# Mixer of a hybrid decoder step: PSUM banks divided 2/2/2/2 instead of 3/2/2/1

## The chip, the core and the metric

The kernel runs on one core of one Trainium2 chip. The metric is the device time of one execution in microseconds. The time before is 2019.17 us, the median of three runs (2019.03 to 2019.56).

## The reference

One decoder layer is applied to a prompt of 1024 positions and to 8 samples of 4 new positions each, 1056 rows of 1024 values:

```python
x = _layer_norm(ALPHA * x + 0.5 * _swiglu(x, ffn1_w_in, ffn1_w_out), ln1_g, ln1_b)
h = x @ w_in
q, k, v, u_b, v_b = jnp.split(h, [D_A, 2 * D_A, 3 * D_A, 3 * D_A + D_B], axis=-1)
# A: 8 heads x 64, windows (128, 512, 2048) at dilations (1, 4, 16), combined by their denominators
# B: u * (W_s LN(v) + b) over chunks of 128 positions, W_s lower-triangular
mixed = jnp.concatenate([_rms_norm(o_a, out_a_g), _rms_norm(o_b, out_b_g)], axis=-1) @ w_out
x = _layer_norm(ALPHA * x + mixed, ln2_g, ln2_b)
x = _layer_norm(ALPHA * x + 0.5 * _swiglu(x, ffn2_w_in, ffn2_w_out), ln3_g, ln3_b)
```

For the samples, the keys and values of 1024 past positions come from a cache. The outputs are the final rows, the key and value rows of the prompt, the shifted caches of the samples and the normalised `v_b` rows of the samples. All of it is float32.

## The kernel before

Three stages follow each other: the first feed-forward block (`ffn(1, ...)`), the mixer (`mixer`), and the output projection with the second feed-forward block. Each dense product is split into a rounded high part and a remainder, so that one product becomes three matmuls on TensorE (`mm3`, line 272).

PSUM has eight banks of 128 x 512 float32. `bank(use)` hands one out. Outside the mixer all eight carry the tag `acc` and are given in turn. In the mixer, `open_banks(self.split)` divides them by use. A bank is free again when its last reader has finished; the next tile of the same tag waits for that.

- `acc` (3 banks): everything that isn't attention proper. The projections of queries and keys (`qk_pair`), of values and of both halves of the gate (`tok_proj`, 24 matmuls into one bank, issued in four parts with other work between them), the gate's spatial product (`mix`, line 943), the transposes of `finish` and `key_rows`, all the work on the samples (`samples`: transposes of cached keys, two score banks s0 and s1 that are held together, transposed probabilities, an output bank), half of the output projection (`out_b`), and the sums for the normaliser (`chunk`, line 1561).
- `sc` (2): scores of the attention (line 1109), read by VectorE with the mask's logarithm added and the row maximum taken (line 1110).
- `pt` (2): probabilities transposed on TensorE (line 1157), then split into high part and remainder by ScalarE and VectorE (lines 1162 to 1169).
- `po` (1): output products of the attention (`pv`, line 1135). One tile collects all key blocks of one head and one 256-wide block of positions; the upper 64 partitions are copied out by ScalarE (line 1143) and added to the lower 64 by VectorE (line 1144). There are 8 heads and 4 blocks, so 32 such tiles.

In `uproj(0)`, for each block of 128 positions, the product's bank stays open while `mix` fills a second one. VectorE adds the bias to mix's result (line 945), and then multiplies the product into it (line 954).

What runs beside what is set by generators. `mixer` walks through `attention`, and for each of its steps advances two others: `dense()` (the projections in the order of `ORDER`) and `windows()` (the samples of the four pairs of heads, once the gate is finished). Each yields an estimated cost, and `ratio`, `ratio2` and `ratio3` set how much of the two is issued for each unit of attention. That gives the order in which the instructions are written. The order in which each engine then gets them is made when the program is built, by the framework's scheduler: it takes the written order as a priority, and an instruction whose tile has no free bank is put back behind others that can go. So the number of banks also has a part in the order of the instructions. The order by hand (`manual_schedule`) is used only for the last rows of the second feed-forward block.

At the end of the mixer, `mix_norm` normalises the attention's result in three chunks of columns, while the last products of `out_b` run.

Of the kernel before, what the change touches and what calls it, by code (L numbers as in the profile page):

```python
# [99 lines left out]
class Net:  # L100
# [1296 lines left out]
            nc.scalar.activation(self.xh[:, 4 + q, :], o[:], AF.Copy)  # L1397
            nc.vector.tensor_sub(self.xl[:, 4 + q, :], o[:], self.xh[:, 4 + q, :].bitcast(F32))  # L1398

    split = {"acc": 3, "sc": 2, "pt": 2, "po": 1}  # L1400
    ratio, ratio2, ratio3 = 5.0, 0.7, 0.7

    def run(self):
# [200 lines left out]
```

## Time and profile before

| what | value |
| --- | --- |
| median of three runs | 2019.17 us |
| the profiled execution | 2019.33 us |
| its span | 2017.5 us |
| instructions | 39560 |
| matmuls | 15775 |
| DMA traffic | 339.65 MB |
| POOL (GpSimd) busy | 140.0 us (7%) |

The profile gives, for one execution, the busy time of each engine: PE is TensorE's matmuls, PEld its weight loads, DVE VectorE, ACT ScalarE, POOL GpSimd and SP SyncE, which issues most DMAs. A group of instructions is named by its line in the kernel, its engine and "out<-in", with the names of the tiles that it writes and reads. Start times are in microseconds from the start of the span. In a row of a timeline, the number in brackets is how long the engine had been idle before the instruction, with the instruction that released it. Matmuls are pipelined, so the duration of a single one is longer than the distance between two.

The mixer lies at about 745 to 1228 us of the span.

### The profile page before, as it was taken

Reading aid. Unit: us, or ns where it says so; the run is one execution under the profiler, and the core shown is the slowest. Engines: PE = TensorE matmul, PEld = TensorE weight load, DVE = VectorE, ACT = ScalarE, POOL = GpSimd, SP = SyncE. Lnnn points to the kernel's source line nnn. Section 1 sums busy time; section 2 is a strip of 40 time slices with the busy share of each in tenths; the row PEclk is TensorE's granted clock in tenths of the full one; section 3 lists DMA queues with packets and bytes.
Section 4 is the critical chain, followed back from the end, with each engine's and each line's share of the span. In section 5 each row is a group of like instructions: output and inputs, shape, how many; then the busy total and the mean of one; then the engine's idle time right before and its main releaser. Section 6 shows DMA issues by size and latency. Waiting matters only on the chain.

```text
span 2017.5 us, 39560 instructions
## 1 busy us (share of the span) xinstructions
PE 1978.6 (98%) x15775; PEld 1919.1 (95%) x15775; DVE 1405.6 (70%) x3196; ACT 825.0 (41%) x1696; POOL 140.0 (7%) x221
## 2 busy tenths in 40 slices
PE   8999999999999999999999899999999999999998
PEld 7999999999999989999898788999999999999997
DVE  5777767777767853846546768767677776777678
ACT  4334333432222373325646653763434343313223
POOL 0000000000000001313213320000000000000003
PEclk9999999999999999999999999999999999999999
DMA  8246454559455243112544755223545655684732
GB/s 236 75 164 214 168 196 170 202 201 346 190 214 193 85 138 102 43 45 87 173 149 141 232 181 177 86 68 103 199 173 192 221 175 196 240 342 143 264 103 108
DMA packets 246823, 339.65 MB, mean 168 GB/s; under 512 B 11699, under 2 KB 205151, under 8 KB 240991
## 3 DMA queue, kind: packets, MB, share of 16 engines
q1 hardware_dynamic: 245399, 333.36, 47.9%
q10 hardware_dynamic: 1240, 3.76, 0.5%
q8 instruction: 124, 2.03, 0.4%
q14 instruction: 60, 0.49, 0.1%
HBM read 238.18 MB, written 132.45 MB: 184 GB/s over the span
## 4 chain that ended last, share of the span: by engine, by line
PE 89%; DVE 6%; DMA 2%; ACT 2%; issue 1%; SPq 0%; POOL 0%; ACTq 0%; DVEq 0%; POOLq 0%
PE acc L511 40%; PE acc L272 21%; PE acc L611 16%; PE acc L479 4%; PE po L1135 2%; PE sc L1109 2%; PE pt L1157 1%; DVE st L376 1%; PE acc L1222 1%; DVE row L791 1%; PE acc L1264 1%; PE acc L305 1%; PE acc L367 0%; DMA tmp<-obT 0%; PE acc L1228 0%
## 5 line engine op out<-in xcount | busy, mean ns | idle before, releaser
L198 ACT ACTIVATE wh<-raw 128x512 fp32r<-128x512 f32 (+1 forms) x528 | 285.3, 551 | 560.0 <-PE acc L611 155.2
L511 PE MATMUL acc<-xo,wh 128*128 128x264 f32 x2560 | 466.7, 283 | 2.3 <-ACT wh L198 1.8
L199 DVE TENSOR_TENSOR wl<-raw,wh 128x512 fp32r<-128x512 f32 (+1 forms) x528 | 311.0, 595 | 130.3 <-ACT wh L198 125.7
L511 PEld LDWEIGHTS acc<-xo,wh 128*128 128x128 f32 x2560 | 394.3, 188 | 3.0 <-ACT wh L198 2.2
L511 PE MATMUL acc<-xo,wl 128*128 128x264 f32 x1280 | 361.2, 283 | 0.0
L511 PE MATMUL acc<-xq,wh 128*128 128x264 f32 x1920 | 350.8, 283 | 0.0
L611 PE MATMUL acc<-gc,wh 128*128 128x264 f32 x1792 | 329.8, 285 | 0.0
L511 PEld LDWEIGHTS acc<-xq,wh 128*128 128x128 f32 x1920 | 295.9, 188 | 0.0
L611 PEld LDWEIGHTS acc<-gc,wh 128*128 128x128 f32 x1792 | 279.3, 189 | 0.2
L511 PE MATMUL acc<-xq,wl 128*128 128x264 f32 x960 | 271.2, 283 | 0.0
L611 PE MATMUL acc<-gc,wl 128*128 128x264 f32 x896 | 255.8, 285 | 0.0
L511 PEld LDWEIGHTS acc<-xo,wl 128*128 128x128 f32 x1280 | 242.0, 189 | 0.0
L511 PEld LDWEIGHTS acc<-xq,wl 128*128 128x128 f32 x960 | 181.6, 189 | 0.0
L611 PEld LDWEIGHTS acc<-gc,wl 128*128 128x128 f32 x896 | 168.5, 188 | 0.0
L272 PE MATMUL acc<-xh,wh 128*128 128x384 f32 (+2 forms) x416 | 134.3, 325 | 4.4 <-ACT xh L1397 2.1
L272 PE MATMUL acc<-xl,wh 128*128 128x384 f32 (+2 forms) x416 | 130.4, 313 | 0.2 <-DVE xl L1398 0.2
L272 PE MATMUL acc<-xh,wl 128*128 128x384 f32 (+2 forms) x416 | 130.0, 313 | 0.0
L272 PE MATMUL acc<-wh,xh 128*128 128x256 f32 (+1 forms) x432 | 122.2, 283 | 0.2 <-ACT tmp L1078 0.2
L272 PE MATMUL acc<-wl,xh 128*128 128x256 f32 (+1 forms) x432 | 121.7, 282 | 0.0
L272 PE MATMUL acc<-wh,xl 128*128 128x256 f32 (+1 forms) x432 | 121.0, 280 | 0.0
L479 PE MATMUL acc<-xq,wh 128*128 128x264 f32 x512 | 99.2, 293 | 3.1 <-ACT wh L198 2.2
L622 DVE TENSOR_TENSOR z<-acc,z 128x264 f32<-128x264 f32 x200 | 83.6, 430 | 21.4 <-PE acc L611 21.0
(223 smaller groups left out, 3558.4 us busy)
## 6 DMA issues: line engine op xcount, KB each, us to landing
gc<-gst SPq DMA_DIRECT2D x112, 528.0 KB
raw<-ffn_w_in SPq DMA_DIRECT2D x88, 512.0 KB
gc<-gc SPq DMA_DIRECT2D x40, 1056.0 KB
raw<-ffn_w_out SPq DMA_DIRECT2D x44, 512.0 KB
gc<-gc SPq DMA_DIRECT2D x32, 528.0 KB
out_ksmp<-cache_k SPq DMA_DIRECT2D x8, 2040.0 KB
out_vsmp<-cache_v SPq DMA_DIRECT2D x8, 2040.0 KB
raw<-w_in SPq DMA_DIRECT2D x20, 512.0 KB
```

What stands on the lines that cost most here:

```text
L198: nc.scalar.activation(h, src, AF.Copy)
L199: nc.vector.tensor_sub(l, src, h.bitcast(F32))
L272: self.nc.tensor.matmul(out, s, m, start=first and i == 0, stop=last and i == n - 1)
L305: nc.tensor.transpose(p[:, r * RB:(r + 1) * RB], t[:RB, k * 128:(k + 1) * 128], self.ident[:RB, :RB])
L376: nc.vector.bn_stats(st[:n, i], ps[i][:n])
L479: nc.tensor.matmul(p, w[:, ks], x[:, z, k % 4], start=k == 0 and q == 0, stop=k == KT - 1 and q == 2)
L511: nc.tensor.matmul(p, w[:, ks], x[:, z, kk], start=new and kk == 0 and r == 0, stop=kk == 3 and r == 2, skip_group_check=True)
L611: nc.tensor.matmul(p, w[:, ks], g[:, o:o + HB], start=new and k == 0, stop=k == nk - 1, skip_group_check=True)
L622: nc.vector.tensor_add(y, p, y)
L791: nc.vector.scalar_tensor_tensor(t[:n, hs], ps[h][:n], mv[:n, 0:1], gb[:n, hs], op0=OP.subtract, op1=OP.mult)
L1109: nc.tensor.matmul(b[:, :w], st[:, i * 128:(i + 1) * 128], kk[:, c0:c0 + w], start=z == 0, stop=z == 1)
L1135: nc.tensor.matmul(out[:, :256], V[p][s][:, 2 * m + kt], x[:, kt], start=m == 0 and kt == 0 and z == 0, stop=m == j and kt == 1 and z == 1)
```

## The change

One line: the mixer's division of the eight banks. The dense products and the samples get two instead of three, the attention's output products two instead of one.

```diff
-    split = {"acc": 3, "sc": 2, "pt": 2, "po": 1}
+    split = {"acc": 2, "sc": 2, "pt": 2, "po": 2}
```

No instruction is added or removed by it, and no tile in SBUF changes. What changes is which bank a tile gets, what it waits for, and through that the order on the engines.

## The prediction

> **What bounds the kernel now.** I read the page's busy times and its chain first, then the mixer alone, since only its PSUM is touched.
>
> ```profile
> PE 1978.6 (98%) x15775; PEld 1919.1 (95%) x15775; DVE 1405.6 (70%) x3196; ACT 825.0 (41%) x1696; POOL 140.0 (7%) x221
> ...
> PE 89%; DVE 6%; DMA 2%; ACT 2%; issue 1%; SPq 0%; POOL 0%; ACTq 0%; DVEq 0%; POOLq 0%
> ```
>
> TensorE is busy 98% of the span, and 89% of the chain that ended last is its work. So time in which TensorE has nothing to issue is paid nearly in full, and a change that removes no work can win only TensorE's idle time. The next view cuts the mixer into stretches (length, then busy time of PE, PEld, DVE, ACT, POOL, the granted clock, DMA share and GB/s):
>
> ```profile
> 745.00:875.00 130.00, 128.20 (x998) 126.39 (x998) 75.55 (x225) 47.23 (x104) 31.79 (x39) 1.00 0.26 79
> ...
> 1110.00:1140.00 30.00, 24.00 (x151) 19.69 (x149) 22.85 (x57) 18.82 (x40) 10.19 (x16) 0.89 0.80 251
> ...
> sum 483.00, PE 469.72 PEld 430.28 DVE 288.05 ACT 236.73 POOL 120.31; mean PE 67.10 PEld 61.47 DVE 41.15 ACT 33.82 POOL 17.19
> ```
>
> In the mixer's 483 us TensorE is idle for 13.3 (483.00 less 469.72); 6.0 of those lie in one hole at 1110 to 1140. What it waits for there (total, times, longest):
>
> ```profile
> PE po L1135 <- DVE oa L1144: 3.1, 4, 1.0
> PE pt L1157 <- DVE pl L1163: 2.6, 3, 1.7
> PE acc L272 <- ACT xh L1397: 2.1, 2, 1.8
> PE acc L1083 <- ACT vo L996: 1.0, 1, 1.0
> ...
> PEld po L1135 <- DVE oa L1144: 4.9, 7, 1.3
> ```
>
> The first row is what the change aims at: an output product waits until L1144 has read the only po bank. It is 3.1 us in four waits; the weight loads' 4.9 us are mostly the same pauses seen one instruction earlier. The fourth row is the longest wait for an acc bank, 1.0 us once: with three of them these waits are covered.
>
> **Part 1, the second po bank.**
>
> ```profile
> L1143 ACT ACTIVATE oadd<-po x32: 380/381/383, 827.8 to 1211.8; 64x256 f32<-64x256 f32 x32
> L1144 DVE TENSOR_TENSOR oa<-po,oadd x32: 396/417/420, 830.8 to 1214.8; 64x256 f32<-64x256 f32 x32
> ```
>
> The po bank is emptied 32 times by a pair of reads of 0.38 and 0.42 us, first to last. That would be 25.6 us if TensorE stood still for each; it stood still 3.1 us, because other instructions lie between. So the gain is bounded by 0 and 4.9 us, and I take the direct row: **-3.1**. No instruction, DMA or SBUF tile is added.
>
> **Part 2, two acc banks: where the third was in use.** Every dense product, transpose and sample score of the mixer draws from acc. I go through the users in the order of the code.
>
> *Plain token products* (values, v half of the gate): bank one is read while bank two is written.
>
> ```profile
> 761.50 22.97 PE acc L272 x192
> ...
> L996 ACT ACTIVATE vo<-acc x16: 359/385/385, 760.6 to 1045.6; 128x256 f32<-128x256 f32 x16
> ```
>
> 192 matmuls in 22.97 us are 0.12 us each, 2.9 us for a product of 24. The read takes 0.385 us. Two banks cover that: **0**.
>
> *The u products of the first half* (`uproj(0)`). After each product comes `mix(n)`, which takes a second bank, and the product's own bank is read only after mix's is (L945, then L954). One of nine such places, TensorE and then VectorE:
>
> ```profile
> 879.78 1.05 PE L943 MATMUL acc<-vb,wt 128*128 128x128 f32 x8
> 880.59 0.36 PE L1135 MATMUL po<-pl,vhl 128*128 128x256 f32 x1
> ...
> 881.02 0.28 PE L272 MATMUL acc<-wh,xh 128*128 128x256 f32 x1
> ```
>
> ```profile
> 880.87 0.69 DVE L945 TENSOR_TENSOR vb<-acc,vec 128x512 f32<-128x512 f32 x1 [2.63 <-PE acc L943]
> 881.59 0.42 DVE L954 TENSOR_TENSOR vb<-acc,vb 128x256 f32<-128x256 f32 x1
> ```
>
> The next product starts at 881.02 in the third bank. With two, the first to come free is mix's, at 881.56 (880.87 and 0.69). Counted from 880.59, when mix has been issued, that is a gap of 0.97 us, nine times: 8.7. Attention work can stand in it: 0.43 us does already here. The stretch of all nine holds this much of it (scores, transposes, outputs; PE busy):
>
> ```profile
> 874.48:913.47 38.99, 2.91 (x13) 1.00 0.19 53
> ```
>
> ```profile
> 874.48:913.47 38.99, 0.98 (x6) 1.00 0.19 53
> ```
>
> ```profile
> 874.48:913.47 38.99, 1.68 (x8) 1.00 0.19 53
> ```
>
> Together 5.57 us. If all of it moved into the gaps, 3.2 us would be left over; if none could, 8.7. I take **+4**, near the lower end, since the instructions are put in order when the program is built, with the bank counts known, and most of the 5.57 us can move a few matmuls.
>
> *The samples.* `samples` takes s0 and s1 together, and VectorE reads them (L1236) when its queue comes to it. One of the eight pairs:
>
> ```profile
> 1066.96 1.28 PE L1228 MATMUL acc<-kv,qbd 128*32 128x512 f32 x16
> ...
> 1069.85 0.29 PE L272 MATMUL acc<-xh,wh 128*128 128x288 f32 x1
> ```
>
> ```profile
> 1072.01 0.67 DVE L1236 CUSTOM_DVE_ANT_0 pt<-acc,pt 128x512 f32<-128x512 f32 x1
> ```
>
> At 1069.85 a dense product runs in the third bank while both others hold scores until 1072.68. With two banks it can't start, and behind an open dense product s1 can't be written until that product has been finished and copied out. I cut out the eight stretches from the last L1228 matmul of a pair to the end of the first L1236 read, for all instructions and then for L272 alone:
>
> ```profile
> sum 39.92, PE 36.38 PEld 32.42 DVE 31.14 ACT 17.50 POOL 12.05; mean PE 4.55 PEld 4.05 DVE 3.89 ACT 2.19 POOL 1.51
> ```
>
> ```profile
> 1011.76:1024.54 12.78, 6.11 (x42) 5.45 (x42) 1.00 0.49 146
> ...
> sum 39.92, PE 15.24 PEld 13.84; mean PE 1.91 PEld 1.73
> ```
>
> In 39.9 us TensorE does 15.2 us of dense work that the change forbids or moves. Upper end: all is lost, 15.2. Lower end: 0, where the open product is drawn ahead of the pair (TensorE stays busy then) and attention fills the rest. Attention can't fill it all: VectorE, on which its next steps wait, is busy 31.14 of 39.92 us. I take half, **+8**.
>
> *The tail.* The normaliser's sum holds a bank while VectorE works through a reciprocal, and an output product waits for its read behind it:
>
> ```profile
> 1212.26 2.54 DVE L1565 RECIPROCAL ry<-ry 128x384 f32<-128x384 f32 x1
> ...
> 1215.76 0.45 DVE L860 SCALAR_TENSOR_TENSOR tmp<-tmp,acc 128x288 f32<-128x288 f32 x1
> ```
>
> ```profile
> 1212.62 3.04 PE L1561 MATMUL acc<-sq,ones 128*128 128x384 f32 x8
> 1215.20 0.63 PE L272 MATMUL acc<-xh,wh 128*128 128x384 f32 x1
> ```
>
> The product at 1215.20 would wait until 1216.21, when L860 has read the one before: 1.0 us. There are three normaliser sums: **+3**, between 0 (VectorE sets the end there, TensorE's wait hides beside it) and 7.6 (a reciprocal of 2.54 each).
>
> *The rest.* The key rows (two transposed blocks and a small one per pair of heads) also use up acc banks in a row:
>
> ```profile
> 876.01 0.60 ACT L1078 ACTIVATE tmp<-acc 128x512 f32<-128x512 f32 x1 [1.82 <-PE acc L1077]
> ```
>
> At most two such reads for four pairs, 4.8 us; mostly attention or the next product can go between: **+1**.
>
> *The clock.* After a pause TensorE has run slower for a while:
>
> ```profile
> 1124.83 0.66 PE L1157 MATMUL pt<-ident,ps 128*128 128x128 f32 x4 [1.67 <-DVE pl L1163]
> ```
>
> ```profile
> 1124.80:1129.00 4.20, 4.17 (x19) 3.89 (x20) 4.17 (x15) 1.34 (x3) 0.48 (x1) 0.59 0.99 331
> ```
>
> After that pause the granted clock is 0.59 for 4.2 us, which costs 1.7 (4.2 times 0.41). New waits of a microsecond or two make one more such spell likely: **+1.7**, from 0 to 5 for three. The Trainium skill, "TensorE: Matmul & The Clock Gate", section "Why this matters for your kernels", sets the limit for a pause at about 3 us; by it the pauses here would leave the clock alone and this term would be 0. The trace differs: the dip follows a recorded pause of 1.67 us, though with thin work around it.
>
> **The sum.** -3.1 + 4 + 8 + 3 + 1 + 1.7 = +14.6 us. The profiled execution took 2019.33 us (span 2017.5), 0.16 above the median of the runs, 2019.17. So 2019.3 + 14.6 = **2034 us**. All upper ends together, without any gain, give 8.7 + 15.2 + 7.6 + 4.8 + 5 = 41 us, 2060; all lower ends, with the gain, 3.2 - 4.9 = -1.7, 2018.
>
> **The rivals.**
>
> A. *Faster.* The order built with two banks draws each dense product together, the po wait goes, and the hole at 1110 to 1140 closes in passing, because the late attention steps fall otherwise against the swap of the activations. -3.1 and up to the hole's 6.0: **2012** with half of the u term (+2). It decides for this side if the acc waits in the mixer stay under some 4 us. For it: the hole is a matter of coincidence. Against it: three banks were live where the u and sample rows stand. The Trainium skill, "Perfetto Trace Analysis", section "Matmuls", has independent products rotate through banks so that a read overlaps the next product; by that rule two for each user are enough, and this rival would hold. The plain products agree with it (0.385 us of read beside 2.9 of product); mix and the sample pairs, which take two banks at once, don't. Chance 0.12.
>
> B. *No change that shows.* Terms of the u products and the samples are covered by reordering and set the po gain off: 3.2 + 1 - 3.1 + 0, **2020**. For it: TensorE has other work, ready or nearly so, all through the mixer (13.3 us idle of 483). Against it: VectorE's 78% in the sample stretches. Chance 0.22.
>
> C. *The sample pairs stop the mixer.* VectorE's queue puts all L1236 reads as late as the third pair's (12.78 us), and dense work of 6.11 us stops eight times: 49 us, less 3.1, with u and tail: **2072**. For it: one pair of eight did so. Against: the other seven are shorter. Chance 0.08.
>
> The forecast keeps 0.58. A measurement of this kernel can tell about 0.2%, 4 us, from no change. Faster by more: A, 0.12. Within: B and the lower edge of the forecast, 0.25. Slower: the rest of the forecast and C, 0.63. The range, 2014 to 2052, takes in B, part of A and most of the unknown costs; it leaves out C and the far end of A.
>
> **What would show it.** In the changed kernel's profile, the wait "po L1135 <- DVE oa L1144" should be gone from TensorE (part 1). Waits of TensorE for L945, L954, L1236 or L860 in acc should appear (u, samples, tail), nine short ones around 880 to 915 and up to eight around the samples. Dense products should lie in longer unbroken runs just ahead of L1228. The two feed-forward stages should keep their lengths; all of the difference must be between 745 and 1228 us. The prediction is wrong if idle time in the mixer stays near 13 us or falls, or if it grows with no wait for a bank's reader.

## The result

The changed kernel takes 2053.35 us (median of four runs, 2050.16 to 2059.84), against 2019.36 for the kernel before measured beside it. The ratio is 1.0174, with a 95% interval from 1.0162 to 1.0187: 34 us slower. The forecast was slower by 14.6 us, 2034, with a range up to 2052. The direction is right; the size is less than half, and the time lies above the range.

The profiled execution took 2053.35 us, of which the span is 2051.5. From its page, the busy times:

```profile
PE 1996.0 (97%) x15775; PEld 1925.1 (94%) x15775; DVE 1406.5 (69%) x3196; ACT 827.3 (40%) x1696; POOL 141.2 (7%) x221
```

Every engine has as many instructions as before. TensorE's busy time rose by 17.4 us (from 1978.6) though its matmuls are the same, and the span by 34.0. So about half of the loss is idle time. The other half is busy time of the same matmuls; a lower clock is a part of it (see below), and the rest was not taken apart. What TensorE waits for in the mixer now (total, times, longest), first its matmuls, then one row for its weight loads:

```profile
PE acc L272 <- DVE tmp L860: 9.4, 5, 4.4
PE acc L272 <- ACT xh L1397: 2.9, 2, 2.5
PE sc L1109 <- DVE mx L1110: 2.7, 4, 1.4
PE acc L1264 <- DMA kv<-cache_v: 2.1, 3, 1.0
PE acc L1222 <- ACT kv L1223: 1.6, 4, 0.6
...
PEld acc L1222 <- ACT kv L1223: 6.8, 23, 0.8
```

The row "po L1135 <- DVE oa L1144" is gone, as part 1 of the forecast said. In its place stand waits for an acc bank: of out_b's products for the read by L860, and of the transposes of the cached keys for ScalarE's copies. Of the four readers that the forecast named, only L860 is among the large waits; L945, L954 and L1236 are not.

The mixer in stretches that begin and end at about the same work, before and after (length, busy time of PE, PEld, DVE, ACT, POOL, granted clock):

```profile
873.00:915.00 42.00, 42.00 (x349) 40.83 (x348) 21.28 (x51) 9.38 (x20) 5.09 (x9) 1.00 0.22 64
...
960.00:1050.00 90.00, 87.07 (x739) 77.31 (x738) 45.31 (x137) 48.73 (x119) 20.77 (x38) 1.00 0.52 155
...
1117.00:1140.00 23.00, 18.48 (x110) 14.85 (x109) 18.46 (x48) 13.04 (x27) 7.17 (x12) 0.85 0.90 287
...
1200.00:1242.00 42.00, 40.05 (x238) 34.64 (x238) 36.03 (x65) 20.72 (x41) 2.10 (x5) 1.00 0.50 167
```

```profile
874.20:923.00 48.80, 47.91 (x385) 45.11 (x384) 32.28 (x84) 17.50 (x39) 10.33 (x18) 1.00 0.18 50
923.00:967.70 44.70, 42.78 (x322) 40.51 (x321) 17.49 (x64) 19.76 (x48) 9.17 (x20) 0.96 0.30 103
967.70:1065.40 97.70, 90.57 (x732) 77.34 (x731) 44.40 (x134) 48.13 (x116) 20.86 (x36) 0.98 0.45 135
...
1132.30:1162.40 30.10, 24.16 (x137) 17.85 (x137) 24.16 (x63) 16.11 (x35) 8.20 (x16) 0.91 0.73 229
...
1222.00:1272.00 50.00, 40.55 (x213) 34.87 (x212) 38.96 (x68) 21.93 (x43) 2.05 (x5) 0.90 0.46 154
```

The loss isn't in one place. The gate takes 6.8 us longer (48.80 against 42.00, though with 36 matmuls more), the first samples 7.7 (97.70 against 90.00, with 7 fewer), the swap 7.1 (27 more), the tail 8.0 (25 fewer). Idle time in these four stretches grew from 9.4 to 23.4 us. The clock column is the second thing to read: length times the missing clock gives 3.5 us before (23.00 times 0.15) and 11.5 after (44.70 times 0.04, 97.70 times 0.02, 30.10 times 0.09, 50.00 times 0.10). Part of that falls in idle time, where a lower clock costs nothing more.

Cut at the first or last start of a line instead, the whole 34.0 us can be laid out (us, in the two profiled executions):

| from, to | before | changed | difference |
| --- | --- | --- | --- |
| start of the span, last L349 (end of the first feed-forward block) | 744.4 | 743.3 | -1.1 |
| to the first mix (L943) | 130.1 | 132.4 | +2.3 |
| to the first transpose of `finish` (L977): the gate | 65.5 | 70.6 | +5.1 |
| to the first key transpose (L1222): `finish` | 20.2 | 21.6 | +1.4 |
| to the last key transpose: the samples, with the swap | 216.2 | 230.8 | +14.6 |
| to the last read by L860: the tail | 61.0 | 71.3 | +10.3 |
| to the end of the span | 780.1 | 781.5 | +1.4 |

As the forecast said, nearly all of the difference lies in the mixer.

### The profile page after: what moved, and what is told of

Read it like the earlier page. It is cut to its first block, busy times and chain, and to the rows that moved or that the text cites. A ratio compares the mean times of both kernels' runs of the same rounds, so it can differ in the third digit from the quotient of the medians.

```text
span 2051.5 us, 39580 instructions
## 1 busy us (share of the span) xinstructions
PE 1996.0 (97%) x15775; PEld 1925.1 (94%) x15775; DVE 1406.5 (69%) x3196; ACT 827.3 (40%) x1696; POOL 141.2 (7%) x221
## 4 chain that ended last, share of the span: by engine, by line
PE 43%; DVE 6%; ACT 2%; DMA 1%; issue 1%; SPq 1%; POOL 0%; ACTq 0%; DVEq 0%
PE acc L511 19%; PE acc L272 9%; PE acc L611 8%; PE acc L479 2%; DVE st L376 1%; PE po L1135 1%; PE acc L1222 1%; PE sc L1109 1%; DVE wl L199 1%; DMA tmp<-obT 1%; PE pt L1157 1%; DVE row L791 1%; DMA kv<-cache_v 1%; PE acc L1264 1%; PE acc L1228 1%
## 5 line engine op out<-in xcount | busy, mean ns | idle before, releaser
L272 PE MATMUL acc<-xh,wh 128*128 128x384 f32 (+2 forms) x416 | 136.7, 330 | 14.0 <-DVE tmp L860 9.4
L272 PE MATMUL acc<-xl,wh 128*128 128x384 f32 (+2 forms) x416 | 133.2, 320 | 0.6 <-DVE xl L1398 0.5
L272 PE MATMUL acc<-xh,wl 128*128 128x384 f32 (+2 forms) x416 | 132.4, 318 | 0.0
L272 PE MATMUL acc<-wh,xh 128*128 128x256 f32 (+1 forms) x432 | 123.9, 287 | 0.8 <-ACT tmp L1078 0.6
L272 PE MATMUL acc<-wl,xh 128*128 128x256 f32 (+1 forms) x432 | 123.0, 285 | 0.0
L272 PE MATMUL acc<-wh,xl 128*128 128x256 f32 (+1 forms) x432 | 122.2, 283 | 0.0
L272 PEld LDWEIGHTS acc<-xh,wh 128*128 128x128 f32 x416 | 80.0, 193 | 19.5 <-DVE tmp L860 9.8
```

The costliest lines, as they stand in the source:

```text
L272: self.nc.tensor.matmul(out, s, m, start=first and i == 0, stop=last and i == n - 1)
```

## The experiments

Theory S: acc banks are scarce wherever something beside an open dense product needs one, and that is the whole loss. Its rivals: the second po bank disturbs the order of the attention (R); VectorE or the caches set the pace in the stretches in question, and the banks only show it (V, D, P).

All ratios are to the kernel before, run beside them. For comparison: the changed kernel's is 1.0174.

**Two acc banks without the second po bank** (`e1`).

```diff
-    split = {"acc": 2, "sc": 2, "pt": 2, "po": 2}
+    split = {"acc": 2, "sc": 2, "pt": 2, "po": 1}
```

> Split 2/2/2/1: acc loses its third bank, po gains nothing, one PSUM bank lies unused. Theory S (the loss is the scarcity of acc banks, and po's second bank gives about 3 us back): 2056 us, between 2050 and 2064, with the waits of po L1135 for oa L1144 back at about 3 us. Rival R (the loss comes from po's second bank, which changes the order of the attention, and two acc banks are enough): within 5 us of before, 2015 to 2025.

Measured: 2052.99 us, ratio 1.0181 (1.0165 to 1.0196). The loss is there without any change to po, so R falls. What the second po bank is worth can't be told: without it the median is 0.4 us lower than the changed kernel's, the ratio 0.0007 (1.4 us) higher, and the intervals overlap almost wholly. The 3 us expected of it don't show. The wait for L1144, in this run:

```profile
PE po L1135 <- DVE oa L1144: 1.1, 2, 0.8
```

It is 1.1 us, not the 3.1 of before and not the 3 expected. That the dense products are held up and VectorE so empties the bank in time is a reading that no run tests.

**Output products sharing pt's banks, acc untouched** (`e4`).

```diff
-    split = {"acc": 3, "sc": 2, "pt": 2, "po": 1}
-    pobank = "po"
+    split = {"acc": 3, "sc": 2, "pt": 3}
+    pobank = "pt"
```

> Before, with acc at 3 and sc at 2, and po's tiles drawn from pt's tag, which has 3 banks: the output products share the transposes' banks, so a second one is at times to be had without a loss for acc. Theory S: faster or equal, 2013 to 2020 us (the po waits of 3.1 us are all that can go). Rival R (letting the output products run ahead itself disturbs the order): 2025 to 2040.

Measured: 2017.21 us, ratio 0.9994 (0.9985 to 1.0004), no difference that can be told; it lies in the range of theory S, and R falls here too. The old wait is replaced by another on the same instructions:

```profile
PE pt L1135 <- DVE pl L1163: 3.7, 5, 1.7
```

So even without a price the gain that the change was after is about 1 us (0.0006 of 2019), and 3 at the edge of the interval. Before, it was the transposes (L1157) that waited for L1163, 2.6 us in three waits, the longest 1.7; here the output products do, and among TensorE's matmuls no transpose waits for L1163 any more. L1163 both makes an operand of the output products and empties a bank of pt, which they now share; the wait row doesn't tell which of the two they wait for.

**The tail: the normaliser's sum from sc** (`e2`).

```diff
         def chunk(c):
             cs = CS[c]
-            b = self.bank()
+            b = self.bank("sc")
```

> The changed kernel (2/2/2/2) with one line different: the normaliser's sum (chunk, L1561) draws its bank from sc, which the attention hardly uses by then. Theory S with its place in the tail (out_b's products wait 9.4 us for L860 because the sum holds one of two acc banks, and two slow-clock spells follow): 2053 less 10 to 13, so 2040 to 2043 us, and no wait of L272 for L860 over 1 us. Rival V (VectorE's reciprocals set the end of the mixer, and TensorE's waits there are hidden beside them): 2050 or more.

Measured: 2042.02 us, ratio 1.0121 (1.0095 to 1.0147), 10.7 us less (0.0053 of 2019). To see why, the changed kernel's TensorE and then VectorE near the end of its mixer:

```profile
1250.20 0.29 PE L272 MATMUL acc<-xh,wl 128*128 128x288 f32 x1
1254.89 0.69 PE L272 MATMUL acc<-xh,wh 128*128 128x384 f32 x1 [4.40 <-DVE tmp L860]
```

```profile
1250.87 1.67 DVE L1572 SCALAR_TENSOR_TENSOR oaT<-oaT,vec,ry 128x384 f32<-128x384 f32 x3
1252.45 1.49 DVE L1574 TENSOR_TENSOR xl<-oaT,xh 128x384 fp32r<-128x384 f32 x3
1253.86 0.61 DVE L1572 SCALAR_TENSOR_TENSOR oaT<-oaT,vec,ry 128x384 f32<-128x384 f32 x1
1254.39 0.45 DVE L860 SCALAR_TENSOR_TENSOR tmp<-tmp,acc 128x288 f32<-128x288 f32 x1
```

A product of out_b is finished at 1250.5, but the read that empties its bank (L860) stands in VectorE's queue behind all of the normaliser's arithmetic and comes at 1254.39. The other acc bank holds the normaliser's next sum, so TensorE has nothing to write to for 4.40 us. And it then runs slower:

```profile
1254.80:1259.40 4.60, 4.51 (x14) 4.51 (x15) 4.51 (x8) 0.62 (x2) 0.00 (x0) 0.50 0.79 249
```

At a clock of 0.50 these 4.6 us cost another 2.3. With the sum in sc, the same tail (from the last output product of the attention to the first result of the projection), changed kernel first:

```profile
1232.40:1272.30 39.90, 30.45 (x151) 26.60 (x150) 32.97 (x56) 15.00 (x30) 0.77 (x1) 0.87 0.45 153
```

```profile
1230.80:1262.10 31.30, 29.10 (x173) 25.97 (x173) 29.79 (x52) 13.15 (x27) 0.77 (x1) 1.00 0.47 158
```

It is 8.6 us shorter with 22 matmuls more in it, and the clock stays at 1.00. It has the length of the kernel before again (1211.20 to 1242.50, 31.30 us), and the waits for L860 are down to two, 1.6 us in all, as expected. The reciprocals are still there, so V falls for the tail: TensorE's waits there were not hidden. What is left of the tail may still be paced by VectorE, which is busy for 29.79 of its 31.30 us.

**The gate: mix from po** (`e5`).

```diff
-            p = self.bank()
+            p = self.bank("po")
             for g in range(4):
```

> The changed kernel with the gate's spatial product (mix, L943) drawn from po instead of acc. Theory S as the forecast had it (each of nine mixes costs the dense products a wait): the stretch from the first to the last mix goes from 43.7 back to about 36 us, and the whole gets 3 to 7 us faster, 2046 to 2050. Rival F (the scheduler fills the gaps with attention that it would have to do later anyway, so nothing is lost there): the stretch gets shorter all the same, but the whole stays within 2 us of the changed kernel's 2053.

Measured: 2044.99 us, ratio 1.0129 (1.0114 to 1.0144), about 9 us less, more than the 3 to 7 expected. The nine mixes and then the rest of the gate up to `finish`, in the kernel before, the changed one and this one:

```profile
874.50:910.40 35.90, 35.90 (x302) 34.89 (x300) 16.99 (x43) 6.92 (x15) 2.86 (x5) 1.00 0.13 39
910.40:940.00 29.60, 29.60 (x249) 29.31 (x249) 18.94 (x63) 13.70 (x34) 9.55 (x14) 1.00 0.12 36
```

```profile
875.70:919.40 43.70, 42.81 (x345) 40.14 (x343) 28.22 (x73) 15.38 (x34) 9.21 (x15) 1.00 0.11 31
919.40:946.30 26.90, 26.90 (x226) 26.64 (x226) 10.68 (x45) 8.61 (x23) 5.34 (x8) 1.00 0.14 41
```

```profile
874.30:910.60 36.30, 36.30 (x302) 35.15 (x301) 17.07 (x43) 6.97 (x16) 2.86 (x5) 1.00 0.13 38
910.60:940.30 29.70, 29.70 (x248) 29.33 (x249) 18.90 (x63) 13.66 (x34) 9.55 (x14) 1.00 0.12 35
```

The gaps were filled, as the forecast hoped: of attention's matmuls, 70 stand in the changed kernel's first stretch instead of 26 (tiles sc, pt and po), and TensorE is idle for 0.89 us only. Still, the two parts together take 70.6 us instead of 65.5, with 20 matmuls more. The rival F, that such filling costs nothing in the end, would have left the whole time within 2 us. It does not hold: the repaired kernel is 8.4 us faster by the medians. In the two profiled executions the gate's two parts hold 4.6 us of this (70.6 against 66.0), `finish` 1.5 (21.6 against 20.1), and 1.4 arise ahead of the first mix, where the edited line has not run yet. The work drawn forward is paid back only in part: from the start of `finish` to the last key transpose the changed kernel has 19 matmuls fewer than this one and still takes 2.1 us longer (252.4 against 250.3). That attention done early is missing there as cover fits this, but no run tests it.

**Sum and mix together** (`e12`): both edits above.

> The changed kernel with the normaliser's sum drawn from sc and mix drawn from po, the two repairs that helped by themselves (11 and 8 us). If the two places are independent: 2053 less 19, 2034 us, between 2031 and 2038. If the tail's waits follow from what happens earlier: less is gained than the sum, 2040 or more.

Measured: 2035.82 us, ratio 1.0084 (1.0061 to 1.0107), 18 us less than the changed kernel's 1.0174 and in the range expected. As far as the intervals can tell, the two places are independent.

**The samples: s1 from po** (`e3`).

```diff
-            s0, s1 = self.bank(), self.bank()
+            s0, s1 = self.bank(), self.bank("po")
```

> The changed kernel with the samples' second score bank s1 drawn from po instead of acc, so that a dense product and a pair of sample scores can be live at once again. Theory S with its place in the samples: less 7 to 14 us, so 2039 to 2046. Rival D (the samples wait for their caches and for VectorE anyway, so the banks are not what holds them): within 3 us of the changed kernel, 2050 to 2056; if s1 blocks the attention's outputs, more.

Measured: 2051.38 us, ratio 1.0166 (1.0149 to 1.0183): no clear gain. The first rows are the changed kernel's `finish` and its first samples, the others the same in this run:

```profile
946.30:967.90 21.60, 19.68 (x127) 17.50 (x126) 9.64 (x30) 12.68 (x30) 4.41 (x13) 0.92 0.59 204
967.90:1061.30 93.40, 86.27 (x700) 73.18 (x699) 41.66 (x130) 45.33 (x111) 20.86 (x36) 0.98 0.46 137
```

```profile
950.10:973.10 23.00, 18.10 (x85) 15.19 (x84) 6.04 (x20) 9.55 (x20) 2.88 (x7) 0.70 0.51 169
973.10:1062.90 89.80, 88.28 (x732) 76.83 (x731) 43.46 (x133) 47.09 (x116) 21.96 (x40) 1.00 0.50 148
```

The samples' stretch is better, 3.6 us shorter with 32 matmuls more; from the first key transpose to the last it is 224.8 us against 230.8. But `finish` has 42 matmuls fewer. TensorE is idle for 4.9 us there, the clock falls to 0.70, and it takes 1.4 us longer. The profiled execution also reached the mixer 3.2 us later (last L349 at 746.5 against 743.3), in a part that the edit doesn't touch. So the time is in the range of rival D, but its reason, that the banks are not what holds the samples, is not shown: some 6 us gained in one stretch don't show in the whole.

**Sum, mix and s1 together** (`e10`).

> As the run with sum and mix, and the samples' second score bank s1 drawn from po as well: all three users that hold two acc banks at once, or one for long, now take the other one elsewhere. Theory S with the forecast's three places: what is left of the loss goes, 2016 to 2026 us. Rival O (what is left in the samples' stretch is the interleaving through one bank of everything else there, and order): as without s1, 2031 to 2038.

Measured: 2032.23 us, ratio 1.0057 (1.0033 to 1.0080). That is 5 us less than without s1 by the ratios, but the intervals overlap. The samples' stretch, from the first key transpose to the last, is 225.4 us against 230.1 without s1 (`e12`), 4.7 us less. Some 11 us of loss remain, as rival O expected, so the pair, which the forecast took for the samples' whole trouble, isn't.

**The key transposes.** In the profile they wait for ScalarE's copy. Their weight loads' idle time (total, times), in the kernel before and in the changed one:

```profile
  ACT kv L1223: 1.0, 3
```

```profile
  ACT kv L1223: 8.4, 27
```

What it looks like in the changed kernel, on TensorE and ScalarE:

```profile
969.18 0.77 PE L1222 MATMUL acc<-ident,kn 128*128 128x128 f32 x5 [0.16 <-ACT kv L1223]
970.53 0.77 PE L1222 MATMUL acc<-ident,kn 128*128 128x128 f32 x5 [0.58 <-ACT kv L1223]
971.87 0.44 PE L272 MATMUL acc<-xh,wh 128*128 128x384 f32 x1 [0.58 <-ACT kv L1223]
```

```profile
969.88 0.77 ACT L1223 ACTIVATE kv<-acc 128x512 f32<-128x512 f32 x2 [0.55 <-PE acc L1222]
971.22 0.77 ACT L1223 ACTIVATE kv<-acc 128x512 f32<-128x512 f32 x2 [0.58 <-PE acc L1222]
```

TensorE and ScalarE take turns: five transposes into the two banks, two copies out, and each stands still meanwhile. Four runs ask whether this is the rest. First, the transposes from po (`e8`), and with sum and mix moved too (`e6`):

```diff
                 for n0, n1 in ((0, 4), (4, 5)):
-                    t = self.bank()
+                    t = self.bank("po")
```

> The changed kernel with the transposes of the cached keys (L1222, 64 tiles) drawn from po instead of acc. Theory K (beside an open dense product these tiles pass through one single bank, and it is there, not at the score pairs, that the samples lose time): the weight loads' wait of L1222 for L1223, 6.8 us in 23 times, falls under 3 us, and the whole gets 4 to 9 us faster, 2044 to 2049. Rival P (score pairs or mere order): under 2 us of change; the drawing of s1 alone from po had given 2.

> The changed kernel with three users moved out of acc at once: the normaliser's sum to sc, mix and the key transposes to po. Theory S with its places (tail 11, samples 4 to 9, gate 0 to 7): 2026 to 2036 us. If the places hang together, so that two banks suffice once the pairs are gone: within 4 us of before, 2015 to 2023. If most of the loss is order alone: 2038 to 2043, as with the sum moved by itself.

Measured: 2066.68 us, ratio 1.0235 (1.0218 to 1.0252), and 2049.23 us, ratio 1.0147 (1.0130 to 1.0164). Both are misses, outside of every range expected: 12 and 13 us slower than the same kernels without this edit. In `e8` the weight loads' wait for L1223 did not fall (6.8 us in 23 times, as in the changed kernel). An output product keeps its po bank through all of its key blocks, so the transposes have one bank at most. Then one bank of their own (`e13`), and that one shared with s1 and mix (`e14`, the sum from sc):

```diff
-    split = {"acc": 2, "sc": 2, "pt": 2, "po": 2}
+    split = {"acc": 2, "sc": 2, "pt": 2, "po": 1, "x": 1}
...
-                    t = self.bank()
+                    t = self.bank("x")
```

> Split 2/2/2/1 (measured at 2053.0) with the eighth bank as a tag of its own for the transposes of the cached keys (L1222). Theory K (in the samples' stretch the loss is these 64 tiles passing through one bank beside an open dense product; drawing them from po only moved the trouble to the output products): 2042 to 2048 us, and the wait of L1222 for L1223 stays or falls, but the score pair no longer holds up dense work. Rival P (it is the score pair): 2050 to 2055.

> Split 2/2/2/1 with the eighth bank shared by the key transposes, the samples' s1 and mix, and the normaliser's sum from sc. Dense products and the rest keep two banks. Theory S in full (the dense products need two banks; the third is for what stands beside them, and that is the whole loss): 2016 to 2024 us. If a part of the loss belongs to the dense products or to the free choice among three banks: 2027 to 2034, as with sum, mix and s1 moved into two po banks (2032).

Measured: 2064.74 us, ratio 1.0220 (1.0204 to 1.0235), and 2037.53 us, ratio 1.0093 (1.0069 to 1.0117). Each is outside of both of its expectations; theory S in full, 2016 to 2024, fails in `e14`. One bank of their own is 8 us worse for the transposes than their share in acc's two (`e13` against `e1`). So the question became whether two of their own are enough. `e15` gives two banks "x" to key transposes, s1 and mix, the sum from sc, and puts the output products into pt's two; `e16` is the same with the key transposes left in acc:

```diff
-    split = {"acc": 2, "sc": 2, "pt": 2, "po": 2}
-    pobank = "po"
+    split = {"acc": 2, "sc": 2, "pt": 2, "x": 2}
+    pobank = "pt"
```

> acc 2 for the dense products and the rest, two banks of their own for key transposes, mix and s1, the sum from sc, and the output products from pt's two banks (which by themselves cost about 6 us: acc 4 with po in pt was 2024). Theory K2 (the key transposes L1222 need two banks beside an open dense product; a single one makes each transposed block wait for ScalarE's copy): 2020 to 2027 us, and L1222's wait for L1223 falls from 8 or 9 us to under 2.5. Rival (a free choice among three or four acc banks is what counts): 2030 or more.

> The same, with the key transposes left in acc (two banks, shared with the dense products). Theory K2: 4 to 12 us slower than the run with them in banks of their own, 2027 to 2036, with L1222's wait for L1223 at 6 to 9 us. Rival: within 2 us of it.

Measured: 2027.23 us, ratio 1.0043 (1.0030 to 1.0056), and 2036.43 us, ratio 1.0088 (1.0063 to 1.0113). Both lie within half a microsecond above the range of K2, and the rival's 2030 or more falls. The two differ by 9 us and in one line, and the wait follows, first `e15`, then `e16`:

```profile
  ACT kv L1223: 1.8, 5
```

```profile
  ACT kv L1223: 4.5, 20
```

The place agrees too. The key transposes of the kernel before, the changed one, `e15` and `e16`, with their first and last start:

```profile
L1222 PE MATMUL acc<-ident,kn x160: 270/272/330, 960.2 to 1176.4; 128*128 128x128 f32 x160
```

```profile
L1222 PE MATMUL acc<-ident,kn x160: 270/273/332, 967.9 to 1198.7; 128*128 128x128 f32 x160
```

```profile
L1222 PE MATMUL x<-ident,kn x160: 270/272/415, 961.3 to 1181.3; 128*128 128x128 f32 x160
```

```profile
L1222 PE MATMUL acc<-ident,kn x160: 270/272/331, 962.3 to 1192.2; 128*128 128x128 f32 x160
```

That is 216.2, 230.8, 220.0 and 229.9 us: the difference of the last two arises between the first and the last of these transposes, while `finish` and the tail of `e15` and `e16` agree within 0.6 us. So it is shown, in this layout, that the key transposes do better with two banks beside the dense products; 9 us is the price of their not having them. The wait recorded in `e16` is lower than the 6 to 9 us expected, and 2.7 us of recorded waits are less than the 9 us of time. In that stretch TensorE's idle time differs by 3.5 us and its busy time by 6.4, with 7 matmuls more in `e16`; so most of the price doesn't show as waiting at all.

**More than before** (`e9`, `e11`). `e9` gives acc four banks and lets po and pt share two; `e11` is `e4` with the sum from sc.

```diff
-    split = {"acc": 3, "sc": 2, "pt": 2, "po": 1}
-    pobank = "po"
+    split = {"acc": 4, "sc": 2, "pt": 2}
+    pobank = "pt"
```

> Before, with acc at 4, sc at 2, and pt and po sharing two banks under one tag. Theory S (what TensorE waits for in the mixer are acc banks, and po's waits are small): 2010 to 2020 us. Rival T (the transposes and output products, sharing two banks, stop each other): 2025 to 2045, with waits of L1157 and L1135 for L1144 of 5 us and more.

> A version that might beat both: acc 3, sc 2, and pt with 3 banks that the output products share, and the normaliser's sum from sc. With the po waits the most that can go (3 us) and 1.0 us of waits for L860 in the tail of before: 2012 to 2018 us, a ratio to before between 0.997 and 1.000. Rival: no difference to before that can be told.

Measured: 2024.27 us, ratio 1.0028 (1.0018 to 1.0037), and 2019.05 us, ratio 0.9995 (0.9981 to 1.0009). `e9` misses both of its expectations: it is slower than before, and the waits of L1157 and L1135 for L1144 are 2.2 us, not 5. For `e11` the rival holds. A fourth acc bank doesn't pay for two banks shared by transposes and output products. Nothing that was run beats the kernel before by more than can be told.

## Why the forecast had the direction and not the size

That two acc banks are too few is right: the loss is there with them alone (`e1`), and comes down where a user finds enough room in other banks (`e2`, `e5`, `e15`). The step that failed is the pricing of the users of acc. The key transposes have no term, the tail and the u products are under-sized, and the gain of part 1 was taken at a wait's full length.

- **Part 1, -3.1.** The wait went, but no gain can be told (`e1` against the changed kernel), and when nothing is paid for it the gain is about 1 us, 3 at the edge of the interval (`e4`). The step took a wait's recorded length for its worth; in `e4` another wait, for L1163, stands on the same instructions.
- **Plain token products, 0.** Nothing contradicts it: no large wait of L272 for L996 appears.
- **The u products, +4 of 3.2 to 8.7.** About 9 by `e5`, 7.5 by `e12` against `e2`; 6 of it in the gate and `finish`. The gaps were filled with attention as forecast, but with 44 matmuls from later, not only with the 5.57 us that stood in the stretch already. What failed is the belief that filled gaps are paid with 0.4 us each: the rest of the gate got 2.7 us shorter by the 23 matmuls that it lost, but `finish` and the samples, with 19 fewer than in `e5`, took 2.1 us longer.
- **The samples, +8 of 0 to 15.2.** The stretch of the samples grew by 14.6 us, near the upper end, and the larger part has another cause. The step put all of it on s0 and s1, whose waits for L1236 hardly appear; s1 alone gave nothing clear (`e3`), and about 5 us beside the other repairs (`e10` against `e12`). The key transposes, a user of acc that the sum put at nothing, cost 9 us (`e15` against `e16`).
- **The tail, +3 of 0 to 7.6.** 10.7 (`e2`). The largest error of a term: one wait of 1.0 us per normaliser sum was read from a product whose read came soon. With two banks the product waits for its turn behind a whole chain of the normaliser's VectorE work, 4.40 us in the longest case, and the slow clock follows. The upper end took only the reciprocal for the chain.
- **The key rows, +1.** No run tests this term. The stretch ahead of the first mix is 2.3 us longer. In it the second transposed block (L1077) waits 1.47 us for a bank that L996 reads, where before the third (L1083) waited 1.03, and the dense product after it waits 0.58 us for L1078 instead of 0.20.
- **The clock, +1.7 of 0 to 5.** By the stretches shown it rose from 3.5 to 11.5 us, by 8, above the term's upper end; part of it lies beside idle time, and it is contained in the places' prices. The step counted one spell because it looked for pauses like the one of 1.67 us. The Trainium skill, "TensorE: Matmul & The Clock Gate", section "Why this matters for your kernels", warns of pauses above about 3 us. The tail's 4.40 us agrees with that, while the clock of 0.92 in `finish` (946.30 to 967.90) has no such pause in it, only 1.92 us of idle time in all.
- **The rivals.** A and B fall: the hole at the swap did not close with the new order, its stretch took 30.10 us instead of 23.00, and waits for acc banks came. C is not what happened either; no pair of scores stopped dense work for long.

Summed up by the ratios, sum and mix together account for 18 of the 35 us (`e12`), s1 for about 5 with overlapping intervals (`e10`), and the key transposes for 9 in a different layout. These 32 us are a sum over layouts, not a run: `e15`, which repairs all four places, is still 9 us slower than before, and what its shared pt banks cost was not measured by itself (`e9`, with two pt banks shared and acc at four, is 6 us slower). So how much is left to the key rows and to the order of the instructions stays open.

## What to carry to other kernels

Before taking a bank from a tag, list everything that draws from it and count, for each, how many banks it needs at once and how long the last reader's queue can hold them; here the loss came from the users beside the main one. Price a bank that hangs on a queue by the whole chain ahead of the read in that queue, not by the read. A recorded wait isn't the price of its cause, in either direction: the removed 3.1 us brought next to nothing, and 2.7 us more of waiting for key transposes came with 9 us of time.

## What was not expected of the hardware

TensorE's clock goes down after thin work, not only after one long pause: it was 0.70 over 23 us in `finish` with 4.9 us of idle time, no pause longer than 1.36 us, and 85 matmuls (`e3`), and 0.50 over 4.6 us behind the 4.40 us pause in the tail. And the key transposes showed on a small scale how much two banks matter: with five transposes per pair of banks, TensorE stood still for 0.58 us out of each 1.34 us (970.53 to 971.87).
